# Emitting the SSM's steps at 1.18 times their pace from the first g_pool tile on, in a one-layer hybrid decoder step

## The chip, the cores and the metric

The kernel runs on one core of a Trainium2 chip. A core has a matrix engine (TensorE, "PE" in the profile; "PEld" is its weight loads), a vector engine (VectorE, "DVE"), an activation engine (ScalarE, "ACT"), GpSimd ("POOL") and SyncE ("SP"). In this kernel POOL and SP mostly issue transfers, which run on 16 shared DMA engines. Each engine works through its own instructions in their order and waits for the others by semaphores. The metric is the device time of one execution in microseconds (us); lower is better.

## What is computed

One layer serves 1024 prompt tokens and 8 x 4 sample tokens, 1056 columns in all, with 1024 features:

```
h    = modulate(rmsnorm(x), shift1, scale1)
u_ssm | u_pool | g_ssm | g_pool = h @ w_in          # 512 | 512 | 1024 | 1024
A    = GLU(gelu(S5(u_ssm)))                         # diagonal complex SSM, 32 groups x 64 states
B    = pooling(u_pool) @ w_pool * pool_scale
x    = x + gate1 * ((sigmoid(g_ssm)*A + sigmoid(g_pool)*B) @ w_out)
x    = x + gate2 * SwiGLU(modulate(rmsnorm(x), shift2, scale2))
y    = rmsnorm(x)
```

The modulation vectors come from `silu(c) @ w_ada`. The S5 part runs a scan over 1024 tokens.

## The kernel before, in words

Features lie on the 128 partitions and tokens along the columns, in three column groups `GROUPS` of 384, 384 and 288. Each fp32 operand is split into a high and a low part (`split`: ACT makes `whi`, DVE makes `wlo`), and `feat` (lines 509 to 511) issues three matmuls for each of 8 feature tiles: a triple. A weight tile of `w_in` with its three groups is called a block here: 24 triples, 72 matmuls, `mm<-hh,whi`, `mm<-hl,whi` and `mm<-hh,wlo` in turn.

The blocks come in this order: 4 for `u_ssm`, 4 for `u_pool` (with the pooling), 8 for `g_pool` (`gated`), 2 of the 8 for `g_ssm` (tiles 6 and 7), then `pump.drain()`, then the other 6 `g_ssm` blocks, the GLU, `w_out` and the feed-forward network.

The S5 part is a generator, `S5.run`. For each quarter q = 0 to 3 of its channels it yields small steps: `gather` (SP reads `U` back from memory), `vk` (DVE makes `vcr`, `vci`; PE multiplies `kp`; POOL writes `Kd` and reads `mt`), `states` (four `vp` products on PE, copied by ACT to `Vr`, `Vi`; then a chain on DVE that makes `Sr` and `Si`), `wrot(q+1)` (DVE makes `wbr`, `wbi`; PE transposes them, `tp`), `tables(q+1)` (DVE), and `outputs(q)` (two groups of `yp` products on PE, lines 377 and 381; ACT copies them to `y`; POOL writes `yd`). So quarter 3 has no `wrot` and no `tables` behind its `states`: its `outputs` come right after.

A `Pump` mixes these steps into the blocks. `feat` calls `tick` after each triple with a nominal time, the Pump subtracts it from `due`, and each time `due` is used up it takes the next step and adds the nominal time that this step yields:

```
    def __call__(self, us):
        if not self.live:
            return
        self.due -= us
        while self.due <= 0:
            try:
                self.due += next(self.gen)
```

`pump.drain()` emits everything that is left, back to back. The order of PE and SP is the order in which the program emits (`manual_schedule`); from the `u_pool` blocks on, a list scheduler orders DVE and ACT when the kernel is built. After the drain the S5 pools are closed and the memory is used again: `gelu(i)` reads `yd` (ACT tiles `ge`, then `gh`), and a second Pump mixes `ada_all` (matmuls of line 608 on pieces of `w_ada`, tile `raw2`, printed as `raw`) into the next blocks. The small tiles of PSUM, `kp`, `tp`, `vp`, `yp` and `aux`, share two buffers.

Of the kernel before, what the change touches and what calls it, by code (L numbers as in the profile page):

```python
# [85 lines left out]
class Later:  # L86


    def __init__(self, eng):
        self.eng, self.kept = eng, []  # L90
# [334 lines left out]
AB, AJ, AN = 2, 2, 3  # L425
GROUPS = ((0, 384), (384, 768), (768, 1056))
ST = 1024


class Pump:  # L430


    def __init__(self, gen):
        self.gen, self.live, self.due = gen, True, 0.0

    def __call__(self, us):
        if not self.live:
            return
        self.due -= us
        while self.due <= 0:  # L440
            try:
                self.due += next(self.gen)
            except StopIteration:
                self.live = False
                return
# [7 lines left out]
def trunk(ctx: ExitStack, tc: tile.TileContext, A, O):  # L453
# [50 lines left out]
    def feat(ps, w, x, g, kts, first=True, last=True):  # L504

        a, b = cols(g)
        for kt in kts:
            (wh, wl), (xh, xl) = w(kt), x(kt)
            pe.matmul(ps, wh, xh[:, a:b], start=first and kt == kts[0], stop=False)  # L509
            pe.matmul(ps, wh, xl[:, a:b], start=False, stop=False)  # L510
            pe.matmul(ps, wl, xh[:, a:b], start=False, stop=last and kt == kts[-1])  # L511
            tick(3 * (b - a) / 2400)

    def mmg(g):
        a, b = cols(g)
        return mm((128, b - a))

    def w8(halves):
        return lambda kt: tuple(h[:, (kt % 4) * 128:(kt % 4) * 128 + 128] for h in halves[kt // 4])
# [73 lines left out]
    def modulate_samples(xs, r, am, ds, k, t):  # L593

        bc = lambda m: m[:, k, None, :].to_broadcast([128, 4, 8])
        f = lambda z: z.rearrange("p (s b) -> p s b", b=8)
        v.tensor_mul(t, xs, r)
        v.tensor_mul(f(t), f(t), bc(am[:, :, 1:9]))
        v.tensor_add(f(t), f(t), bc(ds[:, :, 1:9]))
# [36 lines left out]
    def h_t(kt, a=0, b=NTOK):  # L636
        x, e = X[kt], min(b, ST)
        v.scalar_tensor_tensor(x[:, a:e], x[:, a:e], mod[1][:, kt, 0:1], R[:, a:e], op0=MUL, op1=MUL)
        if b > ST:
            modulate_samples(x[:, ST:], R[:, ST:], mod[1], mod[0], kt, x[:, ST:])  # L640

# [145 lines left out]
    pump = Pump(s5.run())  # L787
# [21 lines left out]
    def pooling(gi, u, out):  # L809
        uv = lambda t: t[:, 0:1024].rearrange("p (j k) -> p j k", k=128)  # L810
        e = ext[gi % 2]
        gp.dma_start(e[:, 0:15, :], A["spool"][gi])
        v.tensor_copy(e[:, 15:19, :], u[:, ST:].rearrange("p (s b) -> p s b", b=8))
        pp = s5p.tile([128, 8, 2], F32, name="pp", tag="pp", bufs=2)
# [6 lines left out]
        while d < win:  # L821
# [6 lines left out]
            else:  # L828
# [9 lines left out]
        v.tensor_sub(uv(cur)[:, :, 0:2], fix, uv(u)[:, :, 0:2])  # L838
        v.scalar_tensor_tensor(cur[:, ST:].rearrange("p (s b) -> p s b", b=8), es[:, 15:19, :], 1.0 / win,
                               e[:, 15:19, :], op0=MUL, op1=SUB)  # L840
# [7 lines left out]
    def pool_map(gi, hl):  # L848
        if gi % 2 == 0:
            t = tmp("wp")  # L850
            nc.sync.dma_start(t, A["w_pool"][:, gi // 2])
            wp[:] = split(t, s5p, "wp", 1)
        for nh in range(2):
            o = (gi % 2) * 256 + nh * 128
            i = 2 * gi + nh
            P[i] = page(f"P{i}")
            for g in range(3):
                ps = mmg(g)
                feat(ps, lambda kt: (wp[0][:, o:o + 128], wp[1][:, o:o + 128]), lambda kt: hl, g, [0])
                act.activation(P[i][:, GROUPS[g][0]:GROUPS[g][1]], ps, AF.Copy, scale=psc[:, i:i + 1])  # L860
# [13 lines left out]
    def gated(i, g, ps):  # L874
        a, b = GROUPS[g]
        t = tmp("sgp")
        act.activation(t[:, 0:b - a], ps, AF.Sigmoid)
        v.tensor_mul(P[i][:, a:b], P[i][:, a:b], t[:, 0:b - a])

    for i in range(8):  # L880
        w = next(wgen)
        for g in range(3):
            ps = mmg(g)
            feat(ps, w8(w), hx, g, range(8))
            if i == 0 and g == 2:
                pool_map(*pend)
            gated(i, g, ps)
# [22 lines left out]
    def gelu(q):  # L910
        hi = pD.tile([128, NTOK], F32R, name=f"gh{q}", tag="gh", bufs=4)
        lo = pD.tile([128, NTOK], F32R, name=f"gl{q}", tag="gl", bufs=4)
        for j0, j1 in ((0, 3), (3, 6), (6, 8)):
# [8 lines left out]
            if j0 < 4:  # L922
                m = min(j1, 4) - j0
                o = [z[:, ST + 8 * j0:ST + 8 * (j0 + m)].rearrange("p (j k) -> p j k", k=8) for z in (hi, lo)]
                act.copy(o[0], tv[:, 0:m, 0:8])
# [3 lines left out]
    def ada_all():  # L929
        units = [(m, hq) for m in (2, 4, 3, 5) for hq in range(4)]  # L930
        qs = [(u, j) for u in units for j in range(4)]

        def fetch(m, hq, j):
            t = pD.tile([128, 512], F32, name="raw2", tag="raw2", bufs=AN)
            nc.sync.dma_start(t, A["w_ada"][m, hq, j // 2, :, j % 2, :])
            return t

        ahead = [fetch(*u, j) for u, j in qs[:AB]]
        yield 5.0
        for i, ((m, hq), j) in enumerate(qs):  # L940
            if j == 0:
                ps = aux((128, 256))
            ada_mm(ps, 2 * j, ahead.pop(0))
            if i + AB < len(qs):
                ahead.append(fetch(*qs[i + AB][0], qs[i + AB][1]))
            if j % AJ == AJ - 1:
                yield 1.7 * AJ
            if j == 3:
                t = tmp("ada")
                act.copy(t[:, 0:256], ps)  # L950
                yield 1.0
                ada_out(m, hq, t, gain[1] if m == 4 else None)

    pump = Pump(ada_all())
# [428 lines left out]
```

## Time and profile before

| what | value |
|---|---|
| time, median of 3 runs | 1340.52 us (1339.44 to 1341.75) |
| the profiled execution's own time | 1340.72 us |
| its span in the trace | 1338.9 us |
| PE busy (share of the span) | 1302.3 us (97%) |
| DVE busy | 776.5 us (58%) |
| ACT busy | 420.1 us (31%) |
| POOL busy | 145.7 us (11%) |
| mean granted TensorE clock | 0.987 of full speed |

The span is the time between the first and the last instruction in the trace; the execution's time is 1.8 us longer. A granted clock of 1.00 is 2.4 GHz, 0.50 is 1.2 GHz.

### The profile page before, as it was taken

How to read it: one execution, taken by the hardware profiler on the slowest of the kernel's cores; microseconds unless marked ns; L12 is line 12 of the kernel's file. 1: busy time of each engine (PE TensorE's matmuls, PEld its weight loads, DVE VectorE, ACT ScalarE, POOL GpSimd, SP SyncE). 2: the span in 40 equal slices, each digit the busy share in tenths (PEclk: the TensorE clock that was granted, in tenths of full speed). 3: DMA queues.
4: the chain of work that ended last, by engine and by line, in shares of the span. 5: the costliest groups of instructions: out<-in, count | busy, mean ns of one | idle time of the engine just before them, and what ended most of it. 6: DMA issues, size and time to landing. Idle time of an engine off the chain costs nothing.

```text
span 1338.9 us, 23073 instructions
## 1 busy us (share of the span) xinstructions
PE 1302.3 (97%) x9276; PEld 1252.2 (94%) x9276; DVE 776.5 (58%) x1805; ACT 420.1 (31%) x801; POOL 145.7 (11%) x289
## 2 busy tenths in 40 slices
PE   7999999999999999999999999999999999999995
PEld 4999999987898999999899999999999999999995
DVE  7987984842115555566966656656666433333357
ACT  5424432333623233233533333333333211111121
POOL 0011112021000000111010110100100321010000
PEclk9999999998999999999999999999999999999997
DMA  9341213033545555112232333333323894333103
GB/s 381 143 135 50 70 51 100 30 89 121 165 146 166 166 175 162 42 65 72 77 113 81 116 112 93 114 100 108 113 89 116 309 358 157 131 110 122 59 13 119
DMA packets 69756, 165.31 MB, mean 123 GB/s; under 512 B 9424, under 2 KB 26000, under 8 KB 69648
## 3 DMA queue, kind: packets, MB, share of 16 engines
q1 hardware_dynamic: 40512, 92.79, 21.5%
q0 software_dynamic: 26688, 68.19, 15.4%
q10 hardware_dynamic: 2448, 2.84, 0.7%
q8 instruction: 73, 1.20, 0.4%
q14 instruction: 35, 0.29, 0.1%
HBM read 125.85 MB, written 37.95 MB: 122 GB/s over the span
## 4 chain that ended last, share of the span: by engine, by line
PE 89%; DVE 6%; issue 1%; ACT 1%; DMA 1%; DVEq 0%; ACTq 0%
PE mm L509 18%; PE mm L511 18%; PE mm L510 18%; PE b L1159 10%; PE b L1158 10%; PE b L1157 10%; PE aux L608 2%; DMA raw<-in_w_ada 1%; PE yp L381 1%; PE vp L320 1%; PE yp L377 1%; PE aux L615 1%; DVE xf L1298 1%; PE aux L588 0%; DVE wlo L489 0%
## 5 line engine op out<-in xcount | busy, mean ns | idle before, releaser
L509 PE MATMUL mm<-hh,whi 128*128 128x384 f32 (+1 forms) x864 | 285.3, 330 | 0.0
L511 PE MATMUL mm<-hh,wlo 128*128 128x384 f32 (+1 forms) x864 | 279.7, 324 | 1.2 <-DVE wlo L489 1.2
L510 PE MATMUL mm<-hl,whi 128*128 128x384 f32 (+1 forms) x864 | 279.9, 324 | 0.9 <-DVE hl L648 0.8
L1159 PE MATMUL b<-th,wlo 128*128 128x264 f32 x640 | 182.2, 285 | 0.0
L1157 PE MATMUL b<-th,whi 128*128 128x264 f32 x640 | 181.8, 284 | 0.0
L1158 PE MATMUL b<-tl,whi 128*128 128x264 f32 x640 | 181.8, 284 | 0.0
L509 PEld LDWEIGHTS mm<-hh,whi 128*128 128x128 f32 x864 | 162.8, 188 | 12.4 <-issue 11.3
L509 PE MATMUL mm<-mh,whi 128*128 128x352 f32 (+3 forms) x528 | 170.7, 323 | 0.0
L511 PE MATMUL mm<-mh,wlo 128*128 128x352 f32 (+3 forms) x528 | 170.4, 323 | 0.0
L510 PE MATMUL mm<-ml,whi 128*128 128x352 f32 (+3 forms) x528 | 170.3, 323 | 0.0
L510 PEld LDWEIGHTS mm<-hl,whi 128*128 128x128 f32 x864 | 163.0, 189 | 1.8 <-DVE hl L648 1.7
L489 DVE TENSOR_TENSOR wlo<-raw,whi 128x512 fp32r<-128x512 f32 (+1 forms) x144 | 90.0, 644 | 128.7 <-ACT whi L488 128.3
L511 PEld LDWEIGHTS mm<-hh,wlo 128*128 128x128 f32 x864 | 162.8, 188 | 1.5 <-DVE wlo L489 1.5
L488 ACT CAST whi<-raw 128x512 fp32r<-128x512 f32 (+1 forms) x144 | 81.2, 585 | 215.0 <-PE mm L510 187.4
L1157 PE MATMUL b<-hh,whi 128*128 128x264 f32 x480 | 136.7, 285 | 3.2 <-ACT p L1202 3.2
L1158 PE MATMUL b<-hl,whi 128*128 128x264 f32 x480 | 137.1, 286 | 0.0
L1159 PE MATMUL b<-hh,wlo 128*128 128x264 f32 x480 | 136.8, 285 | 0.0
L1158 PEld LDWEIGHTS b<-tl,whi 128*128 128x128 f32 x640 | 120.5, 188 | 0.0
L1157 PEld LDWEIGHTS b<-th,whi 128*128 128x128 f32 x640 | 120.3, 188 | 0.0
L1159 PEld LDWEIGHTS b<-th,wlo 128*128 128x128 f32 x640 | 120.2, 188 | 0.0
L509 PEld LDWEIGHTS mm<-mh,whi 128*128 128x128 f32 x528 | 99.4, 188 | 0.9 <-issue 0.2
L510 PEld LDWEIGHTS mm<-ml,whi 128*128 128x128 f32 x528 | 99.4, 188 | 0.5
(340 smaller groups left out, 2162.9 us busy)
## 6 DMA issues: line engine op xcount, KB each, us to landing
raw<-in_w_ada SPq DMA_DIRECT2D x64, 256.0 KB, 3.2
raw<-in_w_in SPq DMA_DIRECT2D x24, 512.0 KB, 4.3
mh<-md POOLq DMA_DIRECT2D x22, 528.0 KB, 8.1
ml<-md POOLq DMA_DIRECT2D x22, 528.0 KB, 8.7
raw<-in_w_ffn_a SPq DMA_DIRECT2D x22, 512.0 KB, 3.5
raw<-in_w_ffn_b SPq DMA_DIRECT2D x22, 512.0 KB, 3.6
md<-mh POOLq DMA_DIRECT2D x40, 264.0 KB, 2.3
md<-ml POOLq DMA_DIRECT2D x40, 264.0 KB, 2.6
```

The lines of the kernel that those rows point to most:

```text
L320: nc.tensor.matmul(vp[64 * g:64 * g + 64, ri, 0:136], wt[:, ri, i, 64 * g:64 * g + 64], U[:, 2 * i + g, 8:144], start=True, stop=True, til ...
L377: nc.tensor.matmul(yps[h][:, k, :], mt[:, 2 * i + h, :], U[:, 2 * i + h, 0:136], start=True, stop=False)
L381: nc.tensor.matmul(yps[h][:, k, :], V[ri][R, i, 1:9, :], S[ri][R, i, 0:136], start=False, stop=ri == 1)
L488: act.copy(hi, raw)
L489: v.tensor_sub(lo, raw, fp(hi))
L509: pe.matmul(ps, wh, xh[:, a:b], start=first and kt == kts[0], stop=False)
L510: pe.matmul(ps, wh, xl[:, a:b], start=False, stop=False)
L511: pe.matmul(ps, wl, xh[:, a:b], start=False, stop=last and kt == kts[-1])
L608: pe.matmul(ps[32 * r:32 * r + 32, :], sil[:, kt, :], w[:, o:o + 256], start=kt < 4, stop=kt >= 4, tile_position=(0, 32 * r))
L1157: pe.matmul(o, wh, xh, start=first and k == 0, stop=False, skip_group_check=True)
L1158: pe.matmul(o, wh, xl, start=False, stop=False, skip_group_check=True)
L1159: pe.matmul(o, wl, xh, start=False, stop=k == 3, skip_group_check=True)
```

## The change

The Pump of the S5 part gets a factor on the nominal time. It is 1.0 at first; in front of the first `g_pool` block it is set to 1.18. Every other Pump keeps 1.0.

```
+RATE = 1.18
...
-        self.gen, self.live, self.due = gen, True, 0.0
+        self.gen, self.live, self.due, self.rate = gen, True, 0.0, 1.0
...
-        self.due -= us
+        self.due -= us * self.rate
...
+    pump.rate = RATE
     for i in range(8):
         w = next(wgen)
         for g in range(3):
```

No instruction of the S5 part is added or removed; the steps are emitted after fewer triples. Lines of the changed kernel stand one further down from the Pump on, and two further down from the `g_pool` loop on (a matmul of line 509 is one of line 510 there, the copies of line 897 are of line 899).

On PE at the drain of the kernel before, behind the last triple of the second `g_ssm` block (288 columns), the `outputs` of quarter 3 begin:

```order
L509 MATMUL mm<-hh_126,whi 128x288
L510 MATMUL mm<-hl_127,whi 128x288
L511 MATMUL mm<-hh_126,wlo 128x288
L377 MATMUL yp<-U,mt 128x136 x2
L381 MATMUL yp<-Sr,vcr 128x136 x2
L381 MATMUL yp<-Si,vci 128x136 x2
```

Both groups of `yp`, 24 products, stand there back to back, and the next block begins behind them. On PE of the changed kernel, at the same triple:

```order
L510 MATMUL mm<-hh_126,whi 128x288
L511 MATMUL mm<-hl_127,whi 128x288
L512 MATMUL mm<-hh_126,wlo 128x288
L510 MATMUL mm<-hh_112,whi 128x384
L511 MATMUL mm<-hl_113,whi 128x384
L512 MATMUL mm<-hh_112,wlo 128x384
```

Nothing of S5 is left at the drain. The `outputs` of quarter 3 now end 53 matmuls ahead of it; this is the end of the first group of `yp` and the start of the second:

```order
L381 MATMUL yp<-Si,vci 128x136 x2
L510 MATMUL mm<-hh_120,whi 128x384
L511 MATMUL mm<-hl_121,whi 128x384
L512 MATMUL mm<-hh_120,wlo 128x384
L510 MATMUL mm<-hh_122,whi 128x384
L511 MATMUL mm<-hl_123,whi 128x384
L512 MATMUL mm<-hh_122,wlo 128x384
L377 MATMUL yp<-U,mt 128x136 x2
```

Two triples now stand between the groups. The distances on PE from the fourth `vp` of a quarter to what follows it change so (matmuls of 384 and of 288 columns between them): to the `tp` behind it in quarter 1, 96 and 48 before, 90 and 27 now; in quarter 2, 96 and 48 before, 75 and 48 now; to the first `yp` of quarter 3, 18 and 24 before, 60 and 27 now.

On ACT the copies of `yp` of quarter 3 (`y`, line 384) stood behind plain work before:

```order
L897 ACTIVATE sg<-mm 128x384
L488 CAST whi<-raw 128x512 x2
L897 ACTIVATE sg<-mm 128x288
L384 COPY y<-yp 128x2x136 x4
L920 CAST gh_3499<-ge 128x384
```

In the changed kernel the scheduler puts `gelu(0)` ahead of them, with four loads of a function table (before, two such loads stood further up, for the same `gelu(0)`):

```order
L918 DMA ge<-yd 128x272
L899 ACT_TABLE_LOAD
L899 ACTIVATE sg<-mm 128x384
L919 ACT_TABLE_LOAD
L919 ACTIVATE ge<-ge 128x272
L899 ACT_TABLE_LOAD
L899 ACTIVATE sg<-mm 128x384
L489 CAST whi<-raw 128x512 x2
L899 ACTIVATE sg<-mm 128x288
L384 COPY y<-yp 128x2x136 x4
```

The first of the four loads stands a few rows ahead of these. The order of POOL is unchanged; on SP two `gather`s move ahead of one load of `w_in` each.

## Rows read from the trace of the kernel before

**Rows 1.** The page: its head line.

```profile
span 1338.9 us, 23073 instructions
```

**Rows 2.** Busy time by window: length, engines with instructions, PEclk, DMA share, GB/s.

```profile
157.00:297.00 140.00, 140.00 (x977) 131.52 (x977) 93.53 (x256) 42.82 (x97) 27.62 (x53) 1.00 0.28 78
...
296.79:313.80 17.01, 12.44 (x59) 10.10 (x58) 8.07 (x24) 3.61 (x11) 3.10 (x6) 0.60 0.11 30
```

**Rows 3.** Waits of PE, 100 to 330 us: total, times, longest.

```profile
PE yp L381 <- DVE Sr L346: 2.7, 1, 2.7
PE yp L381 <- DVE Si L350: 1.3, 1, 1.3
PE tp L265 <- DVE wbi L131: 1.2, 1, 1.2
PE aux L608 <- DMA raw<-in_w_ada: 0.8, 1, 0.8
```

**Rows 4.** Timeline of PE around the drain: start, duration, instruction, idle before.

```profile
296.65 0.30 PE L511 MATMUL mm<-hh,wlo 128*128 128x288 f32 x1
296.79 0.62 PE L377 MATMUL yp<-U,mt 128*128 128x136 f32 x4
...
300.12 0.71 PE L381 MATMUL yp<-Sr,vcr 64*128 64x136 f32 x4 [2.71 <-DVE Sr L346]
...
305.93 1.27 PE L377 MATMUL yp<-U,mt 128*128 128x136 f32 x4 [0.51 <-ACT y L384]
...
310.76 0.69 PE L509 MATMUL mm<-hh,whi 128*128 128x384 f32 x1
...
311.24 0.52 PE L510 MATMUL mm<-hl,whi 128*128 128x384 f32 x1
...
311.56 0.52 PE L511 MATMUL mm<-hh,wlo 128*128 128x384 f32 x1
...
313.80 0.41 PE L509 MATMUL mm<-hh,whi 128*128 128x384 f32 x1
```

**Rows 5.** Timeline of PE: a group of yp of quarter 2.

```profile
264.78 0.62 PE L377 MATMUL yp<-U,mt 128*128 128x136 f32 x4
...
267.33 0.44 PE L509 MATMUL mm<-hh,whi 128*128 128x384 f32 x1
267.61 0.33 PE L510 MATMUL mm<-hl,whi 128*128 128x384 f32 x1
267.78 0.34 PE L511 MATMUL mm<-hh,wlo 128*128 128x384 f32 x1
```

**Rows 6.** Timeline: wbi and its tp in quarter 1, then in quarter 2.

```profile
190.39 0.69 DVE L131 TENSOR_TENSOR wbi<-t,t 128x512 f32<-128x512 f32 x1
...
196.68 0.60 PE L265 MATMUL tp<-ident,wbi 128*128 128x128 f32 x4
...
249.78 0.68 DVE L131 TENSOR_TENSOR wbi<-t,t 128x512 f32<-128x512 f32 x1
...
255.37 0.60 PE L265 MATMUL tp<-ident,wbi 128*128 128x128 f32 x4
```

**Rows 7.** Timeline of quarter 3: the fourth vp, and Si.

```profile
289.72 0.68 PE L320 MATMUL vp<-U,wt 128*64 128x136 f32 x8
...
301.43 0.69 DVE L350 TENSOR_TENSOR Si<-ra,rb 128x512 f32<-128x512 f32 x1
```

**Rows 8.** Timeline of ACT: a table load and what follows it.

```profile
318.07 1.28 ACT L917 ACT_TABLE_LOAD   x1 [0.90 <-issue]
319.37 1.01 ACT L917 ACTIVATE ge<-ge 128x408 f32<-128x408 f32 x2
```

**Rows 9.** DMA issues, 318 to 324 us: count, size, median us to landing.

```profile
raw<-in_w_ada SPq DMA_DIRECT2D x3, 256.0 KB, 4.9
```

**Rows 10.** The same transfers on the page, over the whole span.

```profile
raw<-in_w_ada SPq DMA_DIRECT2D x64, 256.0 KB, 3.2
```

## The prediction

> **What bounds the kernel now.** I read the head and the windows first. PE is busy for all of the 140 us between 157 and 297 us, the stretch in which the S5 steps are mixed into the `g_pool` and `g_ssm` blocks, at a clock of 1.00, while DVE is busy for 93.5 of them [rows 2]. So in that stretch PE alone sets the pace, and emitting steps earlier or later there gains nothing by itself: their work on PE is the same. DVE has room on the mean, not everywhere.
>
> Then the waits. Between 100 and 330 us four waits of PE matter here [rows 3], and the two longest are one place: the `yp` products of quarter 3, which wait 2.7 us for `Sr` and 1.3 us for `Si`. The timeline shows why. The drain emits what is left of the S5 steps in one piece, so `yp` follows the last triple directly, at 296.79, and its operands are not there: PE stands still ahead of 300.12, and later once more for 0.51 us, for the copy to `y` [rows 4]. There is nothing else for PE to do, since its order is the program's.
>
> The window over this place shows the second loss. From 296.79 to 313.80 us PE is busy for 12.44 of 17.01 us, and its mean clock is 0.60 [rows 2]; with the two levels 0.50 and 1.00 that is 0.8 of the stretch, 13.6 us, at half speed. The spacing of the matmuls of the next block says the same: 0.32 us apart at 311.24 and 311.56, against 0.17 us in the middle of the kernel [rows 4, 5]. The full rate is back at 313.80. In the rows the clock is low from the waits on, through work that follows them without a gap.
>
> **The change, part by part.** Between the first `g_pool` block and the drain lie ten blocks and a pool map, so a pace of 1.18 emits the rest of S5 before the drain; in the order of the changed kernel the second group of `yp` ends 53 matmuls ahead of it. No instruction's work changes. What moves is where PE meets results of DVE.
>
> *What is taken away.* The stretch from 296.79 to 313.80 us holds two groups of `yp` and nine matmuls of 384 columns (310.76 up to, not with, 313.80). At full rate a group of `yp` takes 2.55 us, 264.78 to 267.33, and the first matmul behind it 0.28 instead of 0.17 us [rows 5]. So the same work takes 2 x (2.55 + 0.11) + 9 x 0.17 = 6.85 us where nothing waits. The stretch costs 17.01 - 6.85 = 10.16 us too much, 4.57 of them idle and the rest slow clock.
>
> Would `yp` wait at its new place? Before, the fourth `vp` starts at 289.72 and `Si` is there at 302.12, 12.4 us later [rows 7]. Now 60 matmuls of 384 and 27 of 288 columns stand between that `vp` and `yp`; at 0.17 and 0.14 us each (0.14 from 296.65 to 296.79 [rows 4]) and 0.68 us for the `vp`, PE comes to `yp` 14.7 us after it. That leaves 2.3 us. The two triples between the groups take 1.0 us, where before the second group came at once and waited 0.51 us for the copies; so this wait goes too.
>
> *The other wait.* PE also waits 0.8 us for a piece of `w_ada` in the block behind the drain [rows 3]. Those transfers took 4.9 us to land there, where such transfers take 3.2 us on the median of the kernel [rows 9, 10]: they met others, the reads for `gelu(1)` among them. In the changed kernel quarter 3's `yd` is written some 10 us earlier, and ACT can issue the reads for `gelu(1)` earlier in the block. Between keeping 0.8 us and losing all of it I take the whole gain, since 3.2 us is shorter than 4.9 us by more than the wait; the other end, no gain, goes into the range.
>
> *What is moved closer.* The transposes `tp` in quarters 1 and 2 need `wbi`, the end of a long chain on DVE that starts with the copies of the fourth `vp`. In quarter 1 `wbi` is ready at 191.08 and its `tp` comes at 196.68, in quarter 2 at 250.46 and 255.37 [rows 6]: 5.6 and 4.9 us to spare. The chain's own length stays, since it hangs on `vp`; the work of PE in between shrinks by 6 matmuls of 384 and 21 of 288 columns in quarter 1, 4.0 us, and by 21 of 384 in quarter 2, 3.6 us. So 1.6 and 1.3 us are left, and I cost both at nothing; DVE's other work (products with `P`, splits of weights) is what could eat them. If it does, PE waits, and nothing else can run. The nearest row for such a wait is the earlier one of this kind, `tp` for `wbi`, 1.2 us [rows 3]: the bounds are 0 and 2.4 us for the two.
>
> *ACT.* In the changed order `gelu(0)` stands ahead of the copies of `yp`, with four table loads. A load takes 1.28 us, and the next instruction starts 1.30 us after it began [rows 8]. From the fourth `vp` to the end of the first group of `yp` PE has 14.7 + 2.55 = 17.2 us of work; four loads take 5.2 us of ACT, the other rows in between some ten short ones. I cost them at nothing. The Trainium skill, "ScalarE: Activation LUTs", section "What ACT_TABLE_LOAD costs", says otherwise: about 1283 ns for the load and about 1380 ns of drain behind it, 2.66 us for each switch. By that the four cost 10.6 us, an estimate, the copies could come late for the second group of `yp`, and the sum would be about 1 us smaller; the trace has the 1.28 us but no drain behind them.
>
> *The moves on SP and in the transfers* I cost at nothing: the `gather`s still come behind the `yp` that frees `U`, and the weight loads behind them are a whole block ahead of their use.
>
> Sum: 10.16 + 0.81 = 11.0 us. The profiled execution took 1340.72 us around a span of 1338.9 [rows 1], 0.2 us above the median of the runs; against the median, 1340.52 - 10.97 = 1329.6 us, 0.8% faster.
>
> **Rivals.**
>
> *The transposes come late.* For it: DVE is the engine that is behind in this stretch, and 1.3 us is little. Against it: the chain was done 4.9 us early, and its place moves with `vp`. Two waits of up to 1.2 us give up to 1332.0 us.
>
> *`yp` of quarter 3 waits again*, for `Si` or for the copies to `y` behind the table loads: 1.3 us, the size of the old wait for `Si`, gives 1330.9 us; if the clock falls as it did, 6.8 us more (half of 13.6), 1337.7 us. Against it stand the 2.3 us above.
>
> *Slower.* The transposes become what `yp` is now: in quarters 1 and 2 PE waits 2.7 us for `wbi` and the clock stays at half for 13.6 us behind each. That is 2 x (2.7 + 6.8) = 19.0 us, 1348.6 us. It decides from 5.5 us for each on. For it speaks only that the clock fell after a wait of 2.7 us; against it that the whole margin would have to be wrong by 4 us, twice.
>
> *No change*, 1340.5 us: the steps are out ahead of the drain, but PE finds the same wait for the same chain wherever it meets it. The distance of 87 matmuls speaks against it.
>
> **How the numbers follow.** Nothing new waits, 0.68, at 1329.6 us (1330.4 if the 0.8 us stay, a third of this case); late transposes 0.17; late `yp` or copies 0.08; slower 0.04; no change 0.03. The low end is the forecast less the 1.1 us by which the fastest run lay under the median: 1328.4. The high end is the late transposes, 1332.0, with 1.2 us for the spread of the runs above the median: 1333.2. Outside lie the last two cases and the dearer part of the late `yp` and of the transposes. About 0.2%, 2.7 us, is what a measurement of this kernel can tell from no change. Faster by more holds the first two cases and all but the clock part of the third, 0.93; same 0.03; slower 0.04.
>
> **What would show it.** Right: no wait for `Sr` and `Si` on PE; a clock of 1.00 from 157 us to the GLU; the first matmul of the third `g_ssm` block some 10 us earlier after the last one of the second; `yp` of quarter 3 at a group's 2.55 us; no wait of `aux` for `w_ada`. Wrong: waits of `tp` for `wbi` at about 190 and 240 us, a stretch at half clock in the `g_pool` blocks, or a wait of `yp` for `y`.

## The result, and the profile after

The changed kernel takes 1326.76 us, median of 4 runs (1326.58 to 1327.63); the kernel before, on the same chip, 1340.91 us (1339.44 to 1341.75). The ratio is 0.9899, 95% interval 0.9887 to 0.9911: 1.0% faster. The forecast was 1329.6 us with a range of 1328.4 to 1333.2 us, so the direction was right and the time lies below the range, 2.8 us under the forecast. A second set of runs of the same changed kernel gave 1327.24 us beside 1339.83 us, ratio 0.9905 (0.9891 to 0.9918).

The page's head line, which answers to [rows 1]:

```profile
span 1325.8 us, 23073 instructions
```

PE is busy for 1295.0 us of it, where it was busy for 1302.3 before.

The waits of PE from 100 to 330 us in the changed kernel, the answer to [rows 3] (total, times, longest):

```profile
PE tp L265 <- DVE wbi L131: 1.2, 1, 1.2
PE mm L511 <- DVE pl L844: 0.8, 1, 0.8
```

The waits on `Sr`, `Si` and `y` and the one on `w_ada` are gone. What is left was there before: the `tp` row is the early one of quarter 0, and the wait on `pl` was 0.8 us as well. The windows, which answer to [rows 2] (length, busy time of PE, PEld, DVE, ACT and POOL, granted clock, share of the transfers, GB/s):

```profile
157.00:297.00 140.00, 140.00 (x990) 130.73 (x989) 98.66 (x271) 45.44 (x100) 31.20 (x59) 1.00 0.29 84
297.00:330.00 33.00, 32.94 (x226) 29.70 (x225) 6.67 (x17) 16.11 (x34) 1.61 (x4) 1.00 0.41 127
```

In the stretch that held the drain (the second row) PE is busy for 32.94 of 33 us at a clock of 1.00, where it was busy for 12.44 of 17.01 us at 0.60. The timeline of PE around the groups of `yp` of quarter 3, which answers to [rows 4] (start, duration, instruction):

```profile
287.10 0.62 PE L377 MATMUL yp<-U,mt 128*128 128x136 f32 x4
...
289.64 0.45 PE L510 MATMUL mm<-hh,whi 128*128 128x384 f32 x1
...
290.80 0.62 PE L377 MATMUL yp<-U,mt 128*128 128x136 f32 x4
```

No row carries an idle time; the first group takes 289.64 - 287.10 = 2.54 us, as one of quarter 2 did [rows 5]. The fourth `vp` and `Si` in the changed kernel, which answer to [rows 7], and `wbi` with its `tp` in quarters 1 and 2, which answer to [rows 6]:

```profile
272.29 0.68 PE L320 MATMUL vp<-U,wt 128*64 128x136 f32 x8
283.90 0.69 DVE L350 TENSOR_TENSOR Si<-ra,rb 128x512 f32<-128x512 f32 x1
187.76 0.69 DVE L131 TENSOR_TENSOR wbi<-t,t 128x512 f32<-128x512 f32 x1
190.71 0.60 PE L265 MATMUL tp<-ident,wbi 128*128 128x128 f32 x4
240.14 0.68 DVE L131 TENSOR_TENSOR wbi<-t,t 128x512 f32<-128x512 f32 x1
242.04 0.60 PE L265 MATMUL tp<-ident,wbi 128*128 128x128 f32 x4
```

PE comes to `yp` 14.81 us after that `vp`, `Si` is there after 12.30 us: 2.5 us to spare. The transposes have 2.3 and 1.2 us left.

To see where the rest came from I measured three stretches between rows that every version has: from the first `vp` to the first `aux<-r,ada` behind the drain, from there to the first `b` (the matmuls of the feed-forward `pair`s, L1157 before and L1159 after), and from the first to the last `b`.

| | first `vp` | first `aux<-r,ada` | first `b` | last `b` | vp to aux | aux to b | first to last b |
|---|---|---|---|---|---|---|---|
| before | 106.12 | 329.45 | 649.29 | 1063.19 | 223.33 | 319.84 | 413.90 |
| after | 105.98 | 318.30 | 638.67 | 1050.27 | 212.32 | 320.37 | 411.60 |
| after, second profile | 105.79 | 318.08 | 637.93 | 1049.49 | 212.29 | 319.85 | 411.56 |

The drain gave 11.01 us (11.04 in the second profile); the forecast's sum was 10.97. The middle stretch is 0.5 us longer in the first profile and the same in the second. The other 2.3 us came 320 us later, in the first feed-forward pair, which the prediction doesn't mention. There PE, DVE and ACT have the same instructions as before; PE's order is the same too, that of ACT and DVE is not. ACT's timeline in the kernel before, at the start of the pairs (start, duration, instruction, idle before and its releaser):

```profile
652.58 4.37 ACT L1093 CAST th<-bf 128x528 fp32r<-128x528 f32 x8 [1.16 <-DVE bf L1110]
656.86 0.61 ACT L1133 CAST whi<-s 128x512 fp32r<-128x512 f32 x1
657.38 0.61 ACT L1133 CAST whi<-raw 128x512 fp32r<-128x512 f32 x1
657.90 0.59 ACT L1202 COPY p<-b 128x528 f32<-128x528 f32 x1
```

And in the changed kernel:

```profile
641.96 2.24 ACT L1095 CAST th<-bf 128x528 fp32r<-128x528 f32 x4 [1.16 <-DVE bf L1112]
644.11 0.61 ACT L1135 CAST whi<-raw 128x512 fp32r<-128x512 f32 x1
644.63 1.16 ACT L1095 CAST th<-bf 128x528 fp32r<-128x528 f32 x2
645.69 0.59 ACT L1204 COPY p<-b 128x528 f32<-128x528 f32 x1
```

The copy `p<-b` (the product `b1` of the first step) started 5.32 us behind the first of the casts `th`; now it starts 3.73 us behind it. Three casts (two `th`, one `whi`), 1.6 us, are no longer ahead of it. Step 2 of the pair accumulates into `b1` and so has to wait for the copy. PE's timeline before, at the matmul that ends this wait and 16 matmuls later:

```profile
658.54 0.48 PE L1157 MATMUL b<-hh,whi 128*128 128x264 f32 x1 [3.20 <-ACT p L1202]
...
662.11 0.28 PE L1158 MATMUL b<-hl,whi 128*128 128x264 f32 x1
```

and at the same two matmuls after, with a wait for `tl` that follows:

```profile
646.33 0.39 PE L1159 MATMUL b<-hh,whi 128*128 128x264 f32 x1 [1.61 <-ACT p L1204]
...
648.37 0.28 PE L1160 MATMUL b<-hl,whi 128*128 128x264 f32 x1
...
651.21 0.39 PE L1160 MATMUL b<-tl,whi 128*128 128x264 f32 x1 [0.35 <-DVE tl L1096]
```

The windows of the 19 us from just before the first `b`, of before:

```profile
649.00:668.00 19.00, 15.80 (x117) 15.59 (x116) 18.30 (x31) 9.22 (x17) 1.05 (x2) 0.91 0.26 77
```

and of after:

```profile
638.40:657.40 19.00, 17.04 (x137) 16.53 (x136) 19.00 (x33) 9.95 (x18) 1.05 (x2) 1.00 0.27 75
```

The mean clock of 0.91 over 19 us is 2 x 0.09 x 19 = 3.4 us at half speed; the 16 matmuls behind the wait start 0.22 us apart there, where those of the changed kernel start 0.12 us apart. Counted from each kernel's first `b` (649.29 and 638.67), the kernel before is 9.25 - 7.66 = 1.6 us behind at the matmul that ends the wait, and 12.82 - 9.70 = 3.1 us behind 16 matmuls later. So the wait on `p` gives 1.6 us and the clock 1.5; the changed kernel then loses some 0.7 us again, most of it around its own wait for `tl`, and 2.3 us remain.

### The profile page after: what moved, and what is told of

Its sections match the earlier page's. It is cut to its first block, busy times and chain, and to the rows that moved or that the text cites. A ratio compares the mean times of both kernels' runs of the same rounds, so it can differ in the third digit from the quotient of the medians.

```text
span 1325.8 us, 23073 instructions
## 1 busy us (share of the span) xinstructions
PE 1295.0 (98%) x9276; PEld 1246.4 (94%) x9276; DVE 776.8 (59%) x1805; ACT 422.3 (32%) x803; POOL 145.7 (11%) x289
## 4 chain that ended last, share of the span: by engine, by line
PE 89%; DVE 7%; DMA 2%; ACT 1%; issue 1%; DVEq 0%; SPq 0%; ACTq 0%
PE mm L510 18%; PE mm L512 17%; PE mm L511 17%; PE b L1160 10%; PE b L1161 10%; PE b L1159 10%; PE aux L609 1%; PE yp L381 1%; DMA raw<-in_w_ada 1%; PE vp L320 1%; PE yp L377 1%; DVE xf L1300 1%; PE aux L589 0%; PE aux L616 0%; DVE wlo L490 0%
## 5 line engine op out<-in xcount | busy, mean ns | idle before, releaser
L1159 PE MATMUL b<-th,whi 128*128 128x264 f32 x640 | 182.0, 284 | 0.0
L1159 PE MATMUL b<-hh,whi 128*128 128x264 f32 x480 | 135.9, 283 | 1.6 <-ACT p L1204 1.6
L1159 PEld LDWEIGHTS b<-th,whi 128*128 128x128 f32 x640 | 120.4, 188 | 0.1
```

What stands on the lines that cost most here:

```text
L1159: pe.matmul(o, wh, xh, start=first and k == 0, stop=False, skip_group_check=True)
```

## The experiments

Theory A, after these traces: there are two causes that have nothing to do with each other, the drain (11.0 us) and the order of ACT and DVE at the feed-forward start (2.3 us). That order is set when the kernel is built, by a list scheduler that works through a simulated time line; any change of what stands earlier may turn it. Rival B, on the second cause: the 2.3 us come with the drain that is removed. Rival C, on the drain itself: the half clock comes of the narrow `yp` matmuls and not of the waits.

The built programs offer the test: with factors of 1.02, 1.18, 1.21, 1.25 and 1.40 the order at the feed-forward start is that of the changed kernel, with 1.04 to 1.15 and 1.50 that of the kernel before. It does not follow the size of the change.

**Factor 1.02**

```diff
-RATE = 1.18
+RATE = 1.02
```

> The change with a factor of 1.02 in place of 1.18. The order of VectorE and ScalarE at the start of the feed-forward pairs is here that of the changed kernel (the p copy goes ahead of two of the th casts), while the last yp group still stands at the drain and the fourth vp of quarter 3 only 15 feature matmuls earlier than before (15 x 0.163 = 2.4 us). Theory A (two causes: the drain, about 10.5 us, and the order at the feed-forward start, 2.3 us, which has nothing to do with the drain): the wait of b on p is 1.6 us and not 3.2, the clock stays at 1.00 there, so 2.3 us come from there; of the drain's waits of 4.57 us some 2 us are left, so 2 to 8 us more come from the drain, as its clock falls or not. Together 1330 to 1337 us. Rival B (the 2.3 us at the feed-forward start come with the removed drain, not with the order): the wait stays 3.2 us with its half clock, and only the drain's 2 to 8 us are gained.

Measured: 1333.64 us beside 1341.22 us, ratio 0.9949 (0.9936 to 0.9963). The waits of PE from 290 to 330 us, and behind the dots those from 630 to 670 us:

```profile
PE yp L381 <- DVE Si L350: 1.7, 1, 1.7
PE yp L377 <- ACT y L384: 0.5, 1, 0.5
...
PE b L1159 <- ACT p L1204: 1.6, 1, 1.6
```

The window of the drain:

```profile
290.00:316.00 26.00, 23.81 (x146) 21.35 (x145) 12.33 (x29) 7.91 (x19) 5.35 (x10) 0.87 0.28 82
```

Of 4.57 us of waiting at the drain 2.2 are left, and of 13.6 us at half clock 2 x 0.13 x 26 = 6.8. The stretch from `vp` to `aux` takes 217.82 us (106.33 to 324.15), 5.5 less than before. And the pairs take 411.52 us (644.53 to 1056.05): the 2.3 us are there in full, with half of the drain's loss still in place. Rival B falls.

**Factor 1.06**

```diff
-RATE = 1.18
+RATE = 1.06
```

> The change with a factor of 1.06. The order at the start of the feed-forward pairs is that of the kernel before, all of the last yp group still stands at the drain, but the fourth vp is 39 feature matmuls (6.4 us) earlier. Theory A: Sr and Si are then ready when yp asks for them, no wait over 0.6 us is left at the drain, the granted clock stays at 1.00 there, and nearly the whole 10.5 us are gained although no yp group has moved into the products: about 1330.5 us, with the wait of 3.2 us on p still there. Rival B: without a drain the wait on p shrinks too, 1328 us. Rival C (the half clock comes of the narrow yp matmuls, not of the waits): clock 0.5 to 0.6 in the drain, 4 to 5 us gained, 1336 us.

Measured: 1329.81 us (1329.63 to 1329.98), ratio 0.9919 (0.9905 to 0.9932). The waits of PE from 290 to 330 us, and behind the dots those from 630 to 670 us:

```profile
PE yp L377 <- ACT y L384: 0.5, 1, 0.5
...
PE b L1159 <- ACT p L1204: 3.2, 1, 3.2
```

The window of the drain:

```profile
290.00:316.00 26.00, 25.53 (x181) 22.98 (x181) 10.42 (x29) 11.21 (x26) 5.35 (x10) 1.00 0.38 114
```

From `vp` to `aux` it takes 212.54 us (105.95 to 318.49), 10.8 less than before, although both groups of `yp` stand at the drain as they did: it is enough that the fourth `vp` comes 6.7 us earlier (283.02 in place of 289.72) and DVE's chain with it. The same `yp` back to back run at a clock of 1.00, so rival C falls. The pairs take 413.92 us (638.34 to 1052.26), as before.

**Factor 1.15**

```diff
-RATE = 1.18
+RATE = 1.15
```

> The change with a factor of 1.15. All yp groups stand ahead of the drain as in the changed kernel, but VectorE and ScalarE have the order of the kernel before at the start of the feed-forward pairs. Theory A: the wait on p is 3.2 us with a stretch of half clock behind it, and the time is that of the changed kernel plus 2.3 us, about 1329.1 us. Rival B (the order there is not what the 2.3 us hang on): 1326.8 us, as the changed kernel.

Measured: 1329.49 us (1329.23 to 1329.96), ratio 0.9917 (0.9903 to 0.9930). The wait of PE at the feed-forward start:

```profile
PE b L1159 <- ACT p L1204: 3.2, 1, 3.2
```

And the window from 638 to 660 us:

```profile
638.00:660.00 22.00, 18.80 (x142) 18.59 (x141) 19.85 (x33) 9.89 (x19) 1.06 (x2) 0.92 0.27 86
```

`vp` to `aux` takes 212.18 us (106.51 to 318.69), the pairs 413.88 us (638.54 to 1052.42). With the order of the kernel before the change gives 1329.5 us, 0.1 us from the forecast. No run changes that order and nothing else, but between 1.15 and 1.18 the stretch of the drain differs by 0.1 us and the pairs by 2.3.

**Filling the idle time** of the kernel before, in the last `g_ssm` block:

```diff
             act.activation(SG[i][:, GROUPS[g][0]:GROUPS[g][1]], ps, AF.Sigmoid)
+        if i == 7:
+            live, pumps[:] = list(pumps), []
+            feat(mmg(0), w8(w), hx, 0, range(8))
+            pumps[:] = live
```

> The kernel before with 24 more feature matmuls (128x384, into a tile that nobody reads) between the last product and the drain: added work, nothing else. At full rate they take 24 x 0.165 = 4.0 us, about as long as the waits on Sr and Si (2.7 and 1.3 us). Theory A (the 10.5 us of the drain are 4.6 us of idle time and the half clock that comes of it): with the idle time filled the waits on Sr and Si go, the clock stays at 1.00, and the kernel is faster by its added work's cover: 10.5 - 4.0 = 6 to 6.5 us, about 1334.7 us. Rival C (the half clock comes of the narrow yp matmuls or of the place): the clock still falls to 0.5, only idle time is replaced by work, and the time stays near 1341 us.

Measured: 1334.10 us beside 1340.12 us, ratio 0.9954 (0.9940 to 0.9968): 24 matmuls more, and 6.0 us faster. The waits of PE from 290 to 330 us:

```profile
PE yp L377 <- ACT y L384: 0.5, 1, 0.5
```

The window of the drain:

```profile
290.00:316.00 26.00, 25.49 (x177) 23.52 (x176) 14.04 (x31) 7.92 (x19) 6.01 (x12) 1.00 0.32 92
```

`vp` to `aux` takes 216.91 us (106.24 to 323.15), 6.4 less. Theory A gave 6 to 6.5: what the drain cost was idle time and the clock that followed it, and work that fills the gap is cheaper than the gap. (Behind it 2.6 us are lost from `aux` to `b`, 1.6 of them in a new wait of the first `b` for `sa`, and 2.3 us are won back in the pairs. That the extra tile shifts the ring of PSUM tiles may be why; it is not shown. The two nearly cancel, so the whole kernel's 6.0 us is partly luck, the 6.4 us of the stretch are not.)

**Factor 1.40**

```diff
-RATE = 1.18
+RATE = 1.40
```

> The change with a factor of 1.40; the order of VectorE and ScalarE at the feed-forward start is that of the changed kernel. The prediction costed the earlier tp transposes at nothing. From before to 1.18 those of quarter 2 moved 39 feature matmuls (6.4 us) and their margin behind wbi fell by about 3.4 us to 2.2 us, those of quarter 3 moved 81 (13.2 us) and theirs fell by about 3.3 us to 1.6 us. At 1.40 they move 30 and 72 more. If the margin shrinks on at the same pace, PE waits some 0.4 us in quarter 2 and 1.3 us in quarter 3, short enough for the clock to stay at 1.00: 1327.5 to 1329 us. Rival (VectorE's steps move as far as the transposes, and the margin holds): no such wait, 1326.8 us. Second rival: the waits add up with those of vp and yp to over 2 us in one place, the clock falls to half, 1333 us or more.

Measured: 1332.17 us (1331.89 to 1335.96), ratio 0.9947 (0.9933 to 0.9961). The waits of PE from 100 to 330 us:

```profile
PE tp L265 <- DVE wbi L131: 3.7, 3, 1.3
PE vp L320 <- DVE kt L241: 1.2, 1, 1.2
...
PE yp L381 <- DVE Si L350: 0.2, 1, 0.2
```

The window from 157 us on:

```profile
157.00:330.00 173.00, 168.89 (x1175) 156.03 (x1174) 104.27 (x286) 57.38 (x127) 32.90 (x63) 1.00 0.29 87
```

Two waits on `wbi` are new (3.7 less the 1.2 of quarter 0), as the shrinking margins said, and one on `kt` that I had not named: 3.9 us together with the one on `Si`, and `vp` to `aux` takes 217.03 us (106.07 to 323.10), 4.7 us more than at 1.18. The time lies 3 us above the one I expected, and the clock did not fall. The first of the two waits on `wbi` was to be 0.4 us and is 1.2, and the expectation took the smaller margin at 1.18 to be 1.6 us where the rows above give 1.2. (It numbers the quarters by what the transposes prepare, one higher than here.) At 1.18 these 1.2 us are all that is left.

**The copy ahead of all casts**, the first of four attempts to take the remaining wait at the feed-forward start from the changed kernel:

```diff
-        step(b1, 0, 0, True)
         p1 = T("p1")
-        act.copy(p1, view(b1))
+        if k == NS:
+            product(b1, cur[0], 0, True)
+            act.copy(p1, view(b1))
+            more_sums()
+            for q in range(4):
+                put_b(q, 4, bf[q, 4])
+            made.append(next(nxt))
+        else:
+            step(b1, 0, 0, True)
+            act.copy(p1, view(b1))
...
-    more_sums()
     cur += list(first)
-    late = {0: 4, 2: 6}
+    late = {2: 6}
```

> The changed kernel with one edit at the first feed-forward pair: the p copy is emitted right behind the first product, ahead of the eight th casts that stood between them. Theory A: the wait of 1.6 us on p goes, and most of the 0.35 us on tl, so about 1325.0 us, which is faster than both kernels. Rival B: the casts that are now later make steps 3 and 4 wait for tl, and nothing is gained, 1326.8 us or up to 1328.

Measured: 1331.64 us, ratio 0.9934 (0.9921 to 0.9946): 4.9 us slower than the changed kernel. The timeline of ACT at the copy, and behind the dots that of DVE:

```profile
642.77 0.60 ACT L1205 COPY p<-b 128x528 f32<-128x528 f32 x1
...
642.99 2.56 DVE L1112 TENSOR_TENSOR bf<-xr 128x528 f32<-128x528 f32 x4
...
646.66 1.94 DVE L1096 TENSOR_TENSOR tl<-bf,th 128x528 fp32r<-128x528 f32 x3
648.52 0.70 DVE L1215 TENSOR_TENSOR u<-b,p 128x528 f32<-128x528 f32 x1
```

The waits of PE from 630 to 670 us:

```profile
PE b L1160 <- DVE tl L1096: 2.4, 1, 2.4
PE b L1159 <- DVE u L1215: 2.0, 1, 2.0
```

The window from 645 us on:

```profile
645.00:672.00 27.00, 22.59 (x161) 21.98 (x160) 18.81 (x30) 10.03 (x18) 1.82 (x4) 0.87 0.19 60
```

The copy is early and nobody waits for it, but DVE now starts the sums `bf` only at 642.99 (641.23 in the changed kernel), with weight work ahead of `tl` and `u`. The waits there are 4.4 us in place of 2.0, and 2 x 0.13 x 27 = 7.0 us run at half clock. That is slower than either case of the expectation. I had moved ACT's wait and not looked at the engine beside it.

**The second batch of casts one step later**

```diff
-    late = {0: 4, 2: 6}
+    late = {1:4, 2:6}
```

> The changed kernel with the second batch of th casts of the first feed-forward pair called for one step later. The scheduler then puts the p copy behind one th cast fewer (0.55 us): the wait on p falls from 1.6 to about 1.05 us and nothing else moves. Theory A: 1326.2 us. Rival (the tl of step 4 come later and their wait of 0.35 us grows by as much): 1326.8 us. Nothing here can be slower than 1327.5 us, unless the wait moves to u or tl as in the version with p ahead of all casts.

Measured: 1327.06 us, ratio 0.9902 (0.9888 to 0.9915), no difference to the changed kernel. The waits of PE there:

```profile
PE b L1159 <- ACT p L1204: 1.1, 1, 1.1
PE b L1160 <- DVE tl L1096: 1.0, 1, 1.0
```

With one cast fewer ahead of the copy the wait on `p` is 0.5 us shorter, which again puts it down to the casts ahead; the wait on `tl` grows by more. The rival was right.

**Four casts on GpSimd**

```diff
-        act.copy(h, f)
+        (gp.tensor_copy if j == 4 else act.copy)(h, f)
```

> The changed kernel with the th casts of j=4 (four of the eight that stand around the p copy) on GpSimd instead of ScalarE. How long a 128x528 cast takes on GpSimd no trace here shows; it writes 128x512 in a MEMSET in 0.53 us, and the four have some 8 us until step 4 asks for them. If one takes up to 1.5 us, the p copy has 1 us less ahead of it, the wait on p falls from 1.6 to 0.6 us or less and the time is 1325.8 us. Rival: VectorE, which takes its instructions in order, waits for the slower casts, u or tl comes late, and the wait moves to them: 1328 to 1332 us.

Measured: 1327.23 us, ratio 0.9905 (0.9891 to 0.9918), again no difference. The waits of PE there:

```profile
PE b L1159 <- DVE u L1207: 1.8, 1, 1.8
PE b L1159 <- ACT p L1204: 0.6, 1, 0.6
```

The timeline of GpSimd and of DVE, a cast and a subtraction beside it:

```profile
643.18 1.04 POOL L1095 CAST th<-bf 128x528 fp32r<-128x528 f32 x1 [0.62 <-DVE bf L1112]
...
643.66 1.11 DVE L1149 TENSOR_TENSOR s<-raw,s 128x512 f32<-128x512 f32 x1
```

The wait on `p` shrinks as expected, and `u` takes it over: what the rival said, at a time below the one that it gave.

**Four subtractions on GpSimd**

```diff
-        v.tensor_sub(l, f, fp(h))
+        (gp if j == 4 else v).tensor_sub(l, f, fp(h))
```

> The changed kernel with the four subtractions that make tl of j=4 on GpSimd instead of VectorE. Where the th casts of the first feed-forward pair were shortened on ScalarE, the wait only passed from p to u or tl; Theory D is that VectorE, 97% busy from 620 to 641 us, is what bounds this place once p is early. With 4 x 0.62 us off VectorE there, and p behind six th casts and no weight cast, the waits on p, u and tl should fall from 1.95 us together to about 1.1 us: 1325.9 us. Rival: the subtractions on GpSimd take over 1 us each (its casts took 1.04) and hold back VectorE's instructions beside them, as its casts did (a 128x512 subtraction beside one took 1.11 instead of 0.69 us), so the wait is again only moved: 1327 to 1328 us.

Measured: 1327.98 us beside 1339.83 us, ratio 0.9912 (0.9899 to 0.9926); the changed kernel, run beside it, 1327.24 us. The waits are 1.0 us on `p`, 0.9 on `tl` and 0.7 on `u`; one subtraction on GpSimd took from 1.33 to 3.85 us. The rival was right.

In all four the waits on `p`, `u` and `tl` together are 2.1 to 4.4 us, never under the changed kernel's 2.0. DVE is busy for 20.41 of the 21 us from 620 to 641 us. That it is what bounds this place fits all four, but the one that took work from DVE handed it to a slower engine; that stays open, and no version here beats the changed kernel.

**The changed kernel again**

> The changed kernel once more, unchanged, for its spread and a second profile: waits at the drain none, 1.6 us on p and 0.35 us on tl at the feed-forward start, 1326.8 us within 0.5. If its runs lie as close together as those with a factor of 1.06 and 1.15 while those of the kernel before spread over 3 to 4 us, then the half clock of the drain is what varies from run to run, and the difference of the medians over that of the two profiles (14.1 against 13.1 us) is this spread.

Measured: 1327.24 us (1327.02 to 1327.59). Over all comparisons the kernel before ran between 1338.49 and 1342.82 us in 31 runs, the changed kernel between 1326.58 and 1327.63 in 8. The two medians differ by 14.2 us in one set and 12.6 in the other, the mechanisms add up to 11.0 + 2.3 = 13.3. That it is the clock behind the drain that spreads the runs of before fits the spread of 0.4 us with 1.06, but it is not shown. In the nine runs of before beside 1.06 the fastest (1338.49 us) has a mean clock of 0.989 and the slowest (1342.82 us) 0.987; in the nine beside this one, which lie within 1.9 us, that order is not clear. And the version with four subtractions, where PE does not wait at the drain, spreads over 1.9 us too.

## Why the prediction was wrong

*What bounds the kernel* was right: PE sets the pace in the stretch, and the drain is where it stood still.

*What is taken away.* 10.16 us plus 0.81 us for `w_ada`, 10.97, measured 11.0 us from `vp` to `aux`. The size of the second term was right and its reason only in part: the transfers that PE waited for took 4.9 us to land before and 4.2 us now, not the 3.2 us of the median, and the 0.7 us were just enough. The version with added matmuls and that with 1.06 show its two halves: the waits, and the half clock that follows them.

*Would `yp` wait.* 2.3 us to spare by the count of matmuls, 2.5 measured. Nothing waits there, and the copies to `y` are not waited for either.

*What is moved closer.* 1.6 and 1.3 us were worked out, 2.3 and 1.2 measured, and costed at nothing rightly. The factor of 1.40 shows that the danger was real: past these margins PE waits 1.2 and 1.3 us, with the clock at 1.00.

*ACT.* The table loads were hidden. In the changed kernel the timeline of ACT has, between the fourth `vp` and `yp`,

```profile
277.73 1.28 ACT L899 ACT_TABLE_LOAD   x1
279.02 0.49 ACT L899 ACTIVATE sg<-mm 128x384 f32<-128x384 f32 x1
```

The next instruction starts 1.29 us after the load began, as in [rows 8]. The Trainium skill, "ScalarE: Activation LUTs", section "What ACT_TABLE_LOAD costs", adds some 1.38 us of drain to each switch; these rows have the load alone, and the measurement decides.

*The step that failed* is the sum itself, and ahead of it the sentence "What moves is where PE meets results of DVE". I followed that only as far as the drain and the block behind it, and took everything after the GLU to be as it was, so the sum has no term there. But DVE and ACT are ordered by the scheduler from the `u_pool` blocks to the end, so the change moved their order wherever two instructions stood close in its time line, 320 us on too. Its worth there, 2.3 us, was in the trace of before as the only wait of PE between 330 us and the last `b`, 3.2 us on `p` with half a clock behind it; and the order of the changed kernel shows the copy three casts further up. None of the rivals held it, and the low end of the range lies 1.6 us too high. Less these 2.3 us the forecast is 1327.3 us; the two sets of the changed kernel gave 1326.76 and 1327.24. With the factor of 1.15, where the order there stays, the time lies 0.1 us from the forecast and `vp` to `aux` gives 11.15 us: the working of the drain was sound, the list of places was too short. (That 0.1 us is closer than this can be known: the kernel before ran at 1341.22 us beside 1.15, 0.7 above the median that the forecast went by.)

It was luck as well: the same scheduler gives the costlier order at 1.06 and 1.15, and the 2.3 us belong to no property of the change.

## What to carry to other kernels

Where a scheduler orders an engine, a change to one phase can change all later ones: compare the order of each engine to the very end, and look at every place where it differs and PE is known to wait. A wait of PE can cost more than itself: behind 3.2 us on `p` and behind the 4.57 us of the drain the clock fell, and even added work in the gap paid. And before a wait is taken from one engine, look at what the next engine in the same chain has queued: here the wait for ACT's copy was shortened four times, and each time a wait for DVE's `u` or `tl` grew by as much or more.

## What the runs showed of the hardware

The granted clock behind a wait of PE, by window: no fall behind 1.6 us on `p` (0.3 more on `tl`), none behind the three waits of 1.2 to 1.3 us at 1.40; 3.4 us at half behind 3.2 us on `p`; 7.0 us behind 2.0 us on `u` and 2.4 on `tl` with the early copy; 6.8 us behind 1.7 and 0.5 us at the drain with 1.02, where narrow `yp` matmuls surround the waits; 13.6 us with 2.7, 1.3 and 0.5 us at the drain before. The length of a wait alone does not tell what the clock does behind it.

A cast of 128x528 took 0.88 to 1.04 us on GpSimd and 0.63 on ACT (0.55 each in a row of eight, which overlap). Beside one on GpSimd a subtraction of DVE with two operands, 128x512, took 1.11 us in place of 0.69. The Trainium skill, "SBUF — State Buffer", section "Who interferes with whom", has it that such an instruction of DVE contends with one of GpSimd that reads SBUF; this row agrees.
